# Moving where TensorE's operands start in SBUF, and the first bias rows and x loads of a two-block fp32 transformer kernel

## The chip, the cores and the metric

The kernel runs on one core of a Trainium2 chip, as one launch. The metric is device time in microseconds, median of three runs: 2502.96 us (2500.68 to 2505.42) before the change.

## The reference

Two transformer blocks run one after the other on a stream `x` of 256 tokens by 1024 features, all in float32. The first block is one layer: three groups of dilated window attention and a state-space scan side by side, gated and merged, then a SwiGLU feed-forward of 2816 hidden features, then a last norm. The second block is two layers with a second stream `xc` of 256 context tokens; each layer has a feed-forward, an attention mixer over both streams, and another feed-forward, with shifts, scales and gates from a modulation of `c`.

```python
h = x
h = h + hybrid_mixer(rmsnorm(h, norm1_w), ...)       # w_in gives q, k, v, z, xbc, dt, gates
h = h + swiglu(rmsnorm(h, norm2_w), w_ffn_in, w_ffn_out)
x = rmsnorm(h, final_norm_w)
...
for l in range(2):
    x = x + 0.5 * mx[2] * swiglu_2(modulate(rms_norm(x), ...), *ffn1)    # xc likewise
    y, y_c = mixer_l(h, hc, ...)
    x = x + mx[5] * y
    x = x + 0.5 * mx[8] * swiglu_2(modulate(rms_norm(x), ...), *ffn2)    # xc likewise, not in the last layer
```

In the dilated attention a bias is added to the logits before the softmax. It depends on the distance of query and key and on the head alone: `rel_bias[bucket(steps * dilation)]`, 24 heads, three groups of eight.

## The kernel before

**Products.** Features lie on the 128 partitions, tokens along the free axis. A weight slab of 128x1024 floats (eight blocks of 128 rows for 128 output features) is loaded by SP into `wraw` (`load_raw`, L111), rounded by ScalarE into `wh` (L120, type fp32r), and VectorE puts the rest, `wraw` minus `wh`, into `wl` (L121). Activations are split the same way into a high and a low part (`ah` and `al`, in the feed-forwards `hh` and `hl`). `mm3_k` (L134) then makes three products for each block of 128 rows: `wh` with high (L139), `wh` with low (L140), `wl` with high (L141). Weights are the stationary operand (loaded by PEld), activations the moving one. A slab is 24 products into one PSUM tile `pm`.

**Columns.** In the first block only `x` is there: 256 columns. From the second block on the two streams lie side by side in one tile (`self.comb`, `[128, KB, 2, T]`), so that a product takes 512 columns (`acts`, L143). The first three units of such a run, and some at its end, take each stream by itself, 256 columns of the same tile. In the last layer's second half only `x` is left: 256 columns again, of the `x` half of that tile.

**Order.** `run` (L197) takes a list of units and other work. It splits the weights of the coming units ahead (`prepare`), then emits products; the first `head` units are emitted as one batch, block by block. A scheduler orders the instructions of each engine from there, and every engine works through its own list in order. `wraw`, `wh` and `wl` have five buffers each, `pm` four. The dilated attention's units are woven with other work by `weave`.

**Bias rows.** At the start `onehot` (`oh`) and `rel_bias` (`rel`) are loaded by GpSimd's queue, three small products (L478) give a row of 896 values for each of eight heads (`brs`), and one GpSimd DMA writes this to DRAM 32 times over (`brow`, L480, 896 KB), so that `load_bias` (L511) can read it back with a row step one value shorter than a row: this gives the diagonal layout that the logits need. `load_bias` puts four DMAs for each group on SP's queue, the queue of the weights. `oh`, `rel` and `brs` lie in a pool that is closed at once, and the attention's tiles (`q`, `k`, the masks `mk`) take its place. `rpb` are eight more GpSimd DMAs (222 KB each, DRAM to DRAM) for the second layer's second mixer.

**Norm.** The norm's first step adds up squares of the eight blocks of `x` (L309 to L313), sums over partitions by TensorE (L336), takes a root on ScalarE (`rs`, L321), spreads it by TensorE (L344), and `y` (L357) is split into `ah` (L125) and `al` (L126).

**Addresses.** Pools take SBUF from the bottom up. `gap` (L92) takes a number of bytes and writes zeros to them, so that what follows starts elsewhere. In the program as built, the five `wraw` lie at 21696 and on, then `wh` from 42176 and `wl` from 62656, all tiles of 4096 bytes and so at 192 modulo 256 (a block of 128 columns is 512 bytes, which changes nothing). `ah` of the first block lies at 106880, of both streams at 115072, the hidden tiles at 147840 and on: 128 modulo 256, 64 bytes less. The normed scan output (`ynh`, `ynl`) is at 224.

## Time and profile before

| | |
|---|---|
| median of three runs | 2502.96 us (2500.68 to 2505.42) |
| profiled execution, its own time | 2511.2 us |
| its span, first to last instruction | 2509.1 us |
| mean granted TensorE clock | 0.986 |
| TensorE busy | 2440.5 us (97%) |
| weight loads (PEld) busy | 2097.5 us (84%) |
| VectorE busy | 1641.9 us (65%) |
| ScalarE busy | 1067.5 us (43%) |
| moved by DMA | 363.83 MB, mean 145 GB/s |

The table is one execution. A product's length in the trace runs from its issue to its last result; successive products overlap, so their rate is read from the distance of their starts. Times in the rows are counted from the start of the span.

### The profile page before, as it was taken

To read this page: it belongs to the slowest core of one execution; us is meant where nothing else is said; L and a number is where in the kernel's file an instruction comes from. 1 tells how busy PE (TensorE), PEld (TensorE's weight loads), DVE (VectorE), ACT (ScalarE), POOL (GpSimd) and SP (SyncE) were. 2 spreads that over 40 slices of the span, in tenths; PEclk is the share of its full clock that TensorE was granted. 3 is DMA by queue.
4 is the path that set the end of the run, shared out by engine and by line. 5 is a ranking of instruction groups with operands and counts; after the bars stand their busy time and mean duration, and the time that the engine had idled before them with its cause. 6 is when DMAs were issued, how large, how long until landed. Compare 5 with 4: busy or idle time off the path is not lost.

```text
span 2509.1 us, 38385 instructions
## 1 busy us (share of the span) xinstructions
PE 2440.5 (97%) x15104; PEld 2097.5 (84%) x15104; DVE 1641.9 (65%) x3012; ACT 1067.5 (43%) x1934; POOL 20.6 (1%) x30
## 2 busy tenths in 40 slices
PE   6999999999999999999999999999999999999999
PEld 5999899999888888886598888887888888866999
DVE  4667787787855675768757666657545455767555
ACT  4667565545522222536743222243222234555443
POOL 1000000000000000000000000000000000000000
PEclk9999899999999999999899999999999999999999
DMA  8555455676444554331025555434555422332554
GB/s 248 161 154 168 137 168 186 203 250 223 160 155 143 162 177 127 122 125 51 1 68 158 161 160 160 155 97 148 171 166 161 142 87 81 108 91 80 177 185 127
DMA packets 117252, 363.83 MB, mean 145 GB/s; under 512 B 21170, under 2 KB 28658, under 8 KB 117072
## 3 DMA queue, kind: packets, MB, share of 16 engines
q1 hardware_dynamic: 114512, 355.73, 44.8%
q0 software_dynamic: 1280, 3.45, 0.7%
q8 instruction: 119, 1.95, 0.3%
q10 hardware_dynamic: 1280, 2.20, 0.3%
q14 instruction: 61, 0.50, 0.1%
HBM read 359.33 MB, written 3.82 MB: 145 GB/s over the span
## 4 chain that ended last, share of the span: by engine, by line
PE 69%; DVE 4%; ACT 2%; issue 1%; DMA 0%; ACTq 0%; DVEq 0%; SPq 0%
PE pm L139 20%; PE pm L140 20%; PE pm L141 20%; PE pt L1128 1%; PE pa L1035 1%; DVE wl L121 1%; PE pm L1327 1%; PE pt L1059 1%; PE pa L1579 1%; PE pm L1587 1%; DVE al L362 1%; PE pa L1343 1%; DVE y L357 1%; PE pm L1267 1%; PE pa L1304 0%
## 5 line engine op out<-in xcount | busy, mean ns | idle before, releaser
L139 PE MATMUL pm<-ah,wh 128*128 128x256 f32 (+2 forms) x3096 | 1007.7, 328 | 25.3 <-ACT ah L361 11.0
L140 PE MATMUL pm<-al,wh 128*128 128x256 f32 (+2 forms) x3096 | 1001.8, 324 | 1.5 <-DVE al L362 1.5
L141 PE MATMUL pm<-ah,wl 128*128 128x256 f32 (+2 forms) x3096 | 999.9, 324 | 0.0
L120 ACT CAST wh<-wraw 128x1024 fp32r<-128x1024 f32 (+4 forms) x535 | 540.4, 1013 | 1028.8 <-PE pm L140 833.4
L121 DVE TENSOR_TENSOR wl<-wraw,wh 128x1024 fp32r<-128x1024 f32 (+4 forms) x535 | 627.4, 1176 | 245.9 <-ACT wh L120 243.4
L139 PEld LDWEIGHTS pm<-ah,wh 128*128 128x128 f32 (+1 forms) x3096 | 587.2, 191 | 87.4 <-ACT ah L361 12.5
L140 PEld LDWEIGHTS pm<-al,wh 128*128 128x128 f32 (+1 forms) x3096 | 591.2, 191 | 56.1 <-DVE al L362 2.8
L141 PEld LDWEIGHTS pm<-ah,wl 128*128 128x128 f32 (+1 forms) x3096 | 588.8, 190 | 52.9 <-issue 1.7
L140 PE MATMUL pm<-hl,wh 128*128 128x512 f32 (+1 forms) x934 | 316.5, 339 | 0.4 <-DVE hl L126 0.4
L139 PE MATMUL pm<-hh,wh 128*128 128x512 f32 (+1 forms) x934 | 316.0, 338 | 0.7 <-DVE xx L449 0.7
L141 PE MATMUL pm<-hh,wl 128*128 128x512 f32 (+1 forms) x934 | 315.9, 338 | 0.0
L989 DVE SCALAR_TENSOR_TENSOR junk<-wraw,cactc 128x1024 f32<-128x1024 f32 x112 | 137.1, 1224 | 187.7 <-DMA wraw<-w_mod 187.5
L989 DVE SCALAR_TENSOR_TENSOR junk<-wraw,cactx 128x1024 f32<-128x1024 f32 x144 | 176.0, 1222 | 40.9 <-DMA wraw<-w_mod 38.3
L140 PEld LDWEIGHTS pm<-hl,wh 128*128 128x128 f32 x934 | 176.4, 189 | 22.2 <-DVE hl L126 0.6
L139 PEld LDWEIGHTS pm<-hh,wh 128*128 128x128 f32 x934 | 175.7, 188 | 22.4 <-issue 0.8
L141 PEld LDWEIGHTS pm<-hh,wl 128*128 128x128 f32 x934 | 175.6, 188 | 21.5
L125 ACT CAST hh<-g 128x512 fp32r<-128x512 f32 (+1 forms) x113 | 59.3, 526 | 183.8 <-DVE g L419 183.8
L419 DVE TENSOR_TENSOR g<-g,pm 128x512 f32<-128x512 f32 (+1 forms) x113 | 64.0, 566 | 69.8 <-PE pm L141 67.9
L126 DVE TENSOR_TENSOR hl<-g,hh 128x512 fp32r<-128x512 f32 (+1 forms) x113 | 63.8, 566 | 0.3
L449 DVE SCALAR_TENSOR_TENSOR xc<-pm,mcol0c,xc 128x256 f32<-128x256 f32 x56 | 26.9, 481 | 56.0 <-PE pm L141 55.9
L415 ACT ACTIVATE g<-pm 128x512 f32<-128x512 f32 (+1 forms) x116 | 56.0, 487 | 1.4 <-PE pm L141 1.4
L1128 PEld LDWEIGHTS pt<-ident,e 128*128 128x128 f32 x272 | 30.7, 145 | 22.1 <-issue 18.8
(423 smaller groups left out, 2243.4 us busy)
## 6 DMA issues: line engine op xcount, KB each, us to landing
wraw<-w_mod SPq DMA_DIRECT2D x144, 512.0 KB, 3.9
wraw<-f1g SPq DMA_DIRECT2D x44, 512.0 KB, 3.7
wraw<-f1u SPq DMA_DIRECT2D x44, 512.0 KB, 4.2
wraw<-f2g SPq DMA_DIRECT2D x44, 512.0 KB, 3.7
wraw<-f2u SPq DMA_DIRECT2D x44, 512.0 KB, 4.0
wraw<-f1d SPq DMA_DIRECT2D x32, 512.0 KB, 4.2
wraw<-f2d SPq DMA_DIRECT2D x32, 512.0 KB, 3.6
wraw<-w_xbc SPq DMA_DIRECT2D x24, 512.0 KB, 3.6
```

The costliest lines, as they stand in the source:

```text
L120: nc.scalar.copy(h[:, :f], raw[:, :f])
L121: nc.vector.tensor_tensor(lo[:, :f], raw[:, :f], h[:, :f].bitcast(F32), op=ALU.subtract)
L125: self.nc.scalar.copy(h, src)
L126: self.nc.vector.tensor_tensor(lo, src, h.bitcast(F32), op=ALU.subtract)
L139: nc.tensor.matmul(out, h[:, c], ah, start=first, stop=False)
L140: nc.tensor.matmul(out, h[:, c], al, start=False, stop=False)
L141: nc.tensor.matmul(out, lo[:, c], ah, start=False, stop=last)
L415: nc.scalar.activation(half(g["g"], s), p, AF.Silu)
L419: nc.vector.tensor_tensor(t, t, p, op=ALU.mult)
L449: self.nc.vector.scalar_tensor_tensor(x, p, gate, x, op0=ALU.mult, op1=ALU.add)
L989: nc.vector.scalar_tensor_tensor(junk, raw, 1.0, K.cact[s], op0=ALU.mult, op1=ALU.mult, accum_out=K.mcol[layer, s][:, j:j + 1])
L1128: nc.tensor.transpose(p[:, j * 128:(j + 1) * 128], b, K.ident)
```

## The change

It does five things.

- *Addresses.* Both streams' `ah` and `al` get a gap of 64 bytes ahead and start at 192 modulo 256; the pools behind them move along, so that `hh` and `hl` come to 192 too. So the 4,770 products of 512 columns that have `wh` or `wl` (at 192) as weights go from distance 64 to distance 0. In the two feed-forwards that run on `x` alone (the first block's, and the last layer's second) a gap of 192 bytes more brings `hh` and `hl` back to 128, and for the second half of the last layer `self.alone` is a view of the activations' tile that starts 48 floats later, at 128. `ynh` and `ynl` come to 128.
- *Bias rows.* `oh` and `brs` are put into tiles that are used later (`bt`, `ct`). The three products are separate steps in the first `weave`; each group gets its own `brow` in DRAM, written 16 times over (192, 128 and 128 KB). `load_bias` issues eight DMAs of 16 partitions for each group, on GpSimd's queue.
- *x* (and later `xc`) comes in two DMAs of four blocks, one on SP's and one on ScalarE's queue, ahead of `cols` and `ident`.
- A first root of one column loads ScalarE's table for roots ahead of the squares; `na`, an exponential, moves into `dt_evac`.
- `run` prepares, for a run of one stream, one unit more while it stands at the first, and none at the last of the head.

```diff
+        self.gap(p, 64)
+        flat = [p.tile([128, KB * 2 * T], F32R, name="a" + n) for n in "hl"]
+        self.comb = [t.rearrange("p (b s t) -> p b s t", b=KB, s=2) for t in flat]
+        self.alone = [t[:, 48:48 + KB * T].rearrange("p (b t) -> p b t", b=KB) for t in flat]
...
     def new_act(self, s):
+        if self.single:
+            return tuple(self.alone)
...
-        for b in range(KB):
-            self.nc.sync.dma_start(self.X[s][:, b], src[:, b])
+        for b, e in ((0, self.nc.sync), (4, self.nc.scalar)):
+            e.dma_start(self.X[s][:, b:b + 4], src[:, b:b + 4])
...
             j, m = i, 0
+            if not two and i < head:
+
+                j = i + 1 if i + 1 < head else n
+                prepare(i)
...
-    brow = K.dram.tile([32, 8, 896], F32, name="brow")
-    for g, (c0, n) in enumerate(((0, 384), (384, 256), (640, 256))):
-        p = K.pa.tile([128, 512], F32, name="pa")
-        nc.tensor.matmul(p[:8, :n], rel[:, g * 8:(g + 1) * 8], oh[:, c0:c0 + n], start=True, stop=True)
-        nc.vector.tensor_copy(brs[:, c0:c0 + n], p[:8, :n])
-    nc.gpsimd.dma_start(brow.rearrange("q h u -> h q u"), brs.unsqueeze(1).to_broadcast([8, 32, 896]))
-    bctx.close()
+    brow = [K.dram.tile([16, 8, n], F32, name=f"brow{g}") for g, n in enumerate((384, 256, 256))]
...
+    oh, brs = (t.rearrange("p a t -> p (a t)")[:n, :896] for t, n in ((bt, 33), (ct, 8)))
+    nc.gpsimd.dma_start(oh, A["onehot"])
...
+    def bias_row(g):
+        c0, n = ((0, 384), (384, 256), (640, 256))[g]
+
+        def f():
+            p = K.pa.tile([128, 512], F32, name="pa")
+            nc.tensor.matmul(p[:8, :n], rel[:, g * 8:(g + 1) * 8], oh[:, c0:c0 + n], start=True, stop=True)
+            nc.vector.tensor_copy(brs[:, c0:c0 + n], p[:8, :n])
+            nc.gpsimd.dma_start(brow[g].rearrange("q h u -> h q u"), brs[:, c0:c0 + n].unsqueeze(1).to_broadcast([8, 16, n]))
+        return f
...
-        for a in range(0, 128, 32):
-            src = bass.AP(tensor=brow.tensor, offset=brow.offset + c0 + 127 - a, ap=[[8 * 896 - 1, 32], [896, 8], [1, w]])
-            nc.sync.dma_start(t[a:a + 32], src)
+        for a in range(0, 128, 16):
+            src = bass.AP(tensor=brow[g].tensor, offset=brow[g].offset + 127 - a, ap=[[8 * n - 1, 16], [n, 8], [1, w]])
+            nc.gpsimd.dma_start(t[a:a + 16], src)
...
-    items = weave(qkv_units(0), [start, lambda: load_bias(0)], 5, 4)
+    items = weave(qkv_units(0), [bias_row(0), start, bias_row(1), lambda: load_bias(0), bias_row(2)], 3, 2)
...
+    K.gap(K.pool(fctx, "gap1", 1), 192)
...
+        if layer == 1:
+            K.gap(K.pool(fctx, "gap2", 1), 192)
...
+    K.stream("x", A["x"])
     nc.scalar.dma_start(K.cols, A["cols"])
     nc.scalar.dma_start(K.ident, A["ident"])
-    K.stream("x", A["x"])
+
+    nc.scalar.activation(K.small.tile([128, 32], F32, name="v")[:, :1], K.ones[:, 0:1], AF.Sqrt)
```

ScalarE's list from its first weight casts on, before; `wh<-wraw` are casts of weights, `ah` of activations, `rs` is the norm's root and `q` the copy of the first finished product:

```order
L120 CAST wh<-wraw 128x1024 x2
L321 ACT_TABLE_LOAD
L321 ACTIVATE rs<-v 128x2
L120 CAST wh<-wraw 128x1024 x2
L125 CAST ah_230<-y 128x256 x4
L120 CAST wh<-wraw 128x1024
L125 CAST ah_230<-y 128x256 x4
L120 CAST wh<-wraw 128x1024 x4
L534 ACTIVATE q<-pm 128x256
```

And now:

```order
L120 CAST wh<-wraw 128x1024 x5
L330 ACTIVATE rs<-v 128x2
L125 CAST ah_213<-y 128x256 x6
L713 ACT_TABLE_LOAD
L713 ACTIVATE na<-cols 32x1
L125 CAST ah_213<-y 128x256 x2
L120 CAST wh<-wraw 128x1024
L545 ACTIVATE q<-pm 128x256
```

Five casts instead of two stand before the root, six instead of nine before the first copy of a product.

GpSimd's list of DMAs after the three loads, before:

```order
L1630 DMA rpb<-rpb 64x1x889
L480 DMA brow<-brs 8x32x896
L1630 DMA rpb<-rpb 64x1x889
L508 DMA mk_152<-mask 128x128
L508 DMA mk_154<-mask 128x128
L1630 DMA rpb<-rpb 64x1x889 x6
```

And now (`bias_502`, `bias_1434` and `bias_2308` are the three groups' bias tiles):

```order
L519 DMA mk_136<-mask 128x128
L519 DMA mk_138<-mask 128x128
L1643 DMA rpb<-rpb 64x1x889
L508 DMA brow_108<-ct 8x16x384
L508 DMA brow_109<-ct 8x16x256
L527 DMA bias_502<-brow_108 16x8x256 x8
L508 DMA brow_110<-ct 8x16x256
L527 DMA bias_1434<-brow_109 16x8x128 x8
L527 DMA bias_2308<-brow_110 16x8x128 x8
L1643 DMA rpb<-rpb 64x1x889 x7
```

The bias loads stood on SP's list, between the weights of the attention's units; that list now holds weights alone there.

## Rows read from the trace of the kernel before

**Rows 1.** the page's first part: busy time, share of the span and instructions

```profile
PE 2440.5 (97%) x15104; PEld 2097.5 (84%) x15104; DVE 1641.9 (65%) x3012; ACT 1067.5 (43%) x1934; POOL 20.6 (1%) x30
```

**Rows 2.** TensorE groups by shape: busy us, mean ns of one, idle before

```profile
L139 PE MATMUL pm<-ah,wh 128*128 128x256 f32 x1968 | 561.2, 288 | 25.3 <-ACT ah L361 11.0 <-ACT q L534 10.1 <-ACT ah L125 2.0
...
L139 PE MATMUL pm<-ah,wh 128*128 128x512 f32 x1112 | 441.6, 397 | 0.0
...
L139 PE MATMUL pm<-hh,wh 128*128 128x512 f32 x474 | 187.5, 396 | 0.0
...
L139 PE MATMUL pm<-hh,wh 128*128 128x256 f32 x460 | 128.5, 279 | 0.7 <-DVE xx L449 0.7
...
L139 PE MATMUL pm<-ynh,wh 128*128 128x256 f32 x96 | 26.9, 281 | 0.0
```

**Rows 3.** TensorE timeline, 256 columns, from 488 us: start, length

```profile
487.74 0.28 PE L141 MATMUL pm<-ah,wl 128*128 128x256 f32 x1
...
494.09 0.28 PE L140 MATMUL pm<-al,wh 128*128 128x256 f32 x1
```

**Rows 4.** the same, products of 256 columns from 2360 us

```profile
2359.79 0.28 PE L140 MATMUL pm<-al,wh 128*128 128x256 f32 x1
...
2366.38 0.28 PE L139 MATMUL pm<-ah,wh 128*128 128x256 f32 x1
```

**Rows 5.** the same, products of 512 columns from 850 us

```profile
849.74 0.40 PE L139 MATMUL pm<-ah,wh 128*128 128x512 f32 x1
...
862.80 0.40 PE L141 MATMUL pm<-ah,wl 128*128 128x512 f32 x1
```

**Rows 6.** timeline of TensorE round its first long wait

```profile
30.67 0.28 PE L141 MATMUL pm<-ah,wl 128*128 128x256 f32 x1
41.08 0.58 PE L139 MATMUL pm<-ah,wh 128*128 128x256 f32 x1 [10.13 <-ACT q L534]
...
45.09 0.35 PE L139 MATMUL pm<-ah,wh 128*128 128x256 f32 x1
```

**Rows 7.** timeline of ScalarE in that wait: idle before, and what ended it

```profile
34.48 1.04 ACT L120 CAST wh<-wraw 128x1024 fp32r<-128x1024 f32 x1 [11.86 <-DMA wraw<-w_k]
...
39.70 1.04 ACT L120 CAST wh<-wraw 128x1024 fp32r<-128x1024 f32 x1 [0.66 <-DMA wraw<-w_v]
40.65 0.38 ACT L534 ACTIVATE q<-pm 128x256 f32<-128x256 f32 x1
```

**Rows 8.** DMA issues, first 44 us: count, KB each, us to landing

```profile
wraw<-w_k SPq DMA_DIRECT2D x5, 512.0 KB, 10.2
...
rpb<-rpb POOLq DMA_DIRECT2D x8, 222.2 KB, 8.8
xx<-x SPq DMA_DIRECT2D x8, 128.0 KB, 5.3
...
brow<-brs POOLq DMA_DIRECT2D x1, 896.0 KB, 22.3
```

**Rows 9.** waits in the first 75 us: us in total, times, longest

```profile
POOL mk L508 <- DMA brow<-brs: 21.7, 1, 21.7
```

**Rows 10.** stretches from the start: busy us, then granted clock, DMA share, GB/s

```profile
32.00:42.00 10.00, 0.92 (x4) 0.92 (x5) 4.90 (x4) 5.28 (x8) 4.53 (x8) 0.65 0.84 300
42.00:52.00 10.00, 10.00 (x77) 10.00 (x77) 2.45 (x3) 3.27 (x5) 0.00 (x0) 0.84 1.06 282
52.00:62.00 10.00, 10.00 (x91) 10.00 (x90) 4.10 (x4) 4.43 (x8) 0.00 (x0) 1.00 1.02 292
```

**Rows 11.** timeline of all engines up to the first product

```profile
11.24 1.04 ACT L120 CAST wh<-wraw 128x1024 fp32r<-128x1024 f32 x1 [0.56 <-DMA wraw<-w_q]
...
14.89 0.20 ACT L321 ACTIVATE rs<-v 128x2 f32<-128x2 f32 x1
...
17.58 1.22 PE L139 MATMUL pm<-ah,wh 128*128 128x256 f32 x4 [1.01 <-ACT ah L125]
```

**Rows 12.** the tile bias: durations, first and last start

```profile
L576 DVE TENSOR_TENSOR pa<-pa,bias x8: 285/292/300, 70.6 to 96.0; 128x128 f32<-128x128 f32 x8
```

More of the change, by code (lines that the diff above doesn't have):

```diff
@@ L79, in __init__ @@
         self.small = self.pool(ctx, "small", 2)
-        self.comb, self.one_p = None, None
+        self.comb, self.one_p, self.single = None, None, False
         self.ps = ctx.enter_context(tc.tile_pool(name="ps", bufs=4, space=PSUM))
@@ L155, in stream @@
         self.X[s] = self.pool(self.ctx, "act" + s, 1).tile([128, KB, T], F32, name="x" + s)
-        for b in range(KB):
-            self.nc.sync.dma_start(self.X[s][:, b], src[:, b])
+        for b, e in ((0, self.nc.sync), (4, self.nc.scalar)):
+            e.dma_start(self.X[s][:, b:b + 4], src[:, b:b + 4])
     def both_acts(self):
         p = self.pool(self.ctx, "acts", 1)
-        self.comb = [p.tile([128, KB, 2, T], F32R, name="a" + n) for n in "hl"]
+        self.gap(p, 64)
+        flat = [p.tile([128, KB * 2 * T], F32R, name="a" + n) for n in "hl"]
+        self.comb = [t.rearrange("p (b s t) -> p b s t", b=KB, s=2) for t in flat]
+        self.alone = [t[:, 48:48 + KB * T].rearrange("p (b t) -> p b t", b=KB) for t in flat]
     def new_act(self, s):
+        if self.single:
+            return tuple(self.alone)
         if self.comb:
@@ L463, in linear @@
         return K.lin(src, i, K.acts, lambda s, p: evac(p), m)
-    bctx = ExitStack()
-    bp = K.pool(bctx, "b1b", 1)
-    oh = bp.tile([33, 896], F32, name="oh")
-    nc.gpsimd.dma_start(oh, A["onehot"])
-    rel = bp.tile([33, 24], F32, name="rel")
-    nc.vector.memset(rel, NEG)
-    nc.gpsimd.dma_start(rel[:32], A["rel_bias"])
-    brs = bp.tile([8, 896], F32, name="brs")
-    brow = K.dram.tile([32, 8, 896], F32, name="brow")
-    for g, (c0, n) in enumerate(((0, 384), (384, 256), (640, 256))):
-        p = K.pa.tile([128, 512], F32, name="pa")
-        nc.tensor.matmul(p[:8, :n], rel[:, g * 8:(g + 1) * 8], oh[:, c0:c0 + n], start=True, stop=True)
-        nc.vector.tensor_copy(brs[:, c0:c0 + n], p[:8, :n])
-    nc.gpsimd.dma_start(brow.rearrange("q h u -> h q u"), brs.unsqueeze(1).to_broadcast([8, 32, 896]))
-    bctx.close()
+    rel = xpool.tile([33, 24], F32, name="rel")
+    nc.vector.memset(rel, NEG)
+    brow = [K.dram.tile([16, 8, n], F32, name=f"brow{g}") for g, n in enumerate((384, 256, 256))]
     tri = K.cst.tile([128, 128], F32, name="tri")
-    nc.gpsimd.dma_start(tri, A["tri"])
     cw = xpool.tile([128, 128], F32, name="cw")[:, :120]
-    K.gap(xpool, 160)
+    K.gap(xpool, 320)
     K.gap(xpool, 352)
@@ L495, in block1 @@
     ao_l = xpool.tile([128, 4, T], F32R, name="aol")
+    K.gap(xpool, 192)
     mst = xpool.tile([128, 3, 2, 8], F32, name="mst")
@@ L498, in block1 @@
     big = lambda name: xpool.tile([128, 8, T], F32, name=name, tag="big")
+    oh, brs = (t.rearrange("p a t -> p (a t)")[:n, :896] for t, n in ((bt, 33), (ct, 8)))
+    nc.gpsimd.dma_start(oh, A["onehot"])
+    nc.gpsimd.dma_start(rel[:32], A["rel_bias"])
+    nc.gpsimd.dma_start(tri, A["tri"])
+    def bias_row(g):
[6 more added lines that the diff above has]
+        return f
     DIL = (1, 4, 16)
@@ L511, in load_bias @@
     def load_bias(g):
[L512 removed]
+        w, n = ((256, 384), (128, 256), (128, 256))[g]
         t = bias[g] = big("bias0") if g == 0 else hp.tile([128, 8, w], F32, name=f"bias{g}", tag="bias", bufs=2)
[L514 to L516 removed]
+        for a in range(0, 128, 16):
+            src = bass.AP(tensor=brow[g].tensor, offset=brow[g].offset + 127 - a, ap=[[8 * n - 1, 16], [n, 8], [1, w]])
+            nc.gpsimd.dma_start(t[a:a + 16], src)
         if g:
@@ L696, in block1 @@
     ladr = K.dram.tile([2, 32, 128], F32, name="ladr")
-    na = xpool.tile([32, 1], F32, name="na")
     def dt_evac(p):
@@ L701, in dt_evac @@
         v, u, w, c = (K.t1(n, (32, T)) for n in ("dv", "du", "dw", "dc"))
+        na = K.t1("na", (32, T))[:, 0:1]
         nc.scalar.activation(na, K.col("a_log", 0, slice(0, 32)), AF.Exp)
@@ L1536, in outputs @@
     def outputs():
+        K.single = True
         K.ACT["x"] = K.new_act("x")
```

1 line of the change is left out of this document (removed).

## The prediction

> **What bounds the kernel now.** I read the page's first part, then TensorE's groups by shape, then its timeline in steady stretches, then the waits of the first 75 us. TensorE is busy 97% of the span [rows 1]. Nearly all of it is one pattern, three products for each block of 128 rows: `wh` with the high part of the activations (L139), `wh` with the low part (L140), `wl` with the high part (L141). Counting each line three times, [rows 2] give (1112 + 474) x 3 = 4,758 products of 512 columns, and thousands of 256 columns. A length there is from issue to drain, and the products overlap, so what counts is the distance between starts. Each of [rows 3 to 5] shows the first and the last of 57 successive rows, 56 steps apart: (494.09 - 487.74) / 56 = 113.4 ns for 256 columns, (2366.38 - 2359.79) / 56 = 117.7 ns for 256 columns elsewhere, and (862.80 - 849.74) / 56 = 233.2 ns for 512 columns. No engine is waited for in these stretches: 256 columns have two levels with the same operand distance, and 512 have one.
>
> What would be free of any stall? After the first long wait, 19 products of 256 columns start from 41.08 to 45.09 us, 211 ns apart [rows 6], while the granted clock is 0.84 over the ten microseconds that hold them [rows 10]: the lower level, 1.2 GHz, at which 256 columns one a cycle take 213 ns. So at 2.4 GHz 512 columns need 213.3 ns, and the 233.2 hold 20 ns of something else; 256 columns need 106.7 and hold 6.7 or 11.0.
>
> The second bound is local. TensorE stands still from 30.67 + 0.12 to 41.08 us, 10.3 us, and the release is the copy of a finished product, `q` [rows 6]. It is not ScalarE's speed: `q` stands in ScalarE's queue behind four weight casts, the first of which waited 11.86 us for a weight transfer [rows 7]. Weights take 10.2 us to land then, since one `brow` write of 896 KB takes 22.3 us among them [rows 8]; GpSimd stands 21.7 us behind it [rows 9].
>
> **The change, part by part.** The sum is made against the profiled execution, 2511.2 us (span 2509.1), which lies 8.2 us over the median of the three runs, 2502.96; a difference found in the one is taken off the other.
>
> *The start.* The `brow` write becomes three (16 copies in place of 32: 192 + 128 + 128 KB, half the bytes), the bias loads go from SP's queue to GpSimd's, seven of the eight `rpb` writes go behind them, and on ScalarE three of the nine casts that stood before the first `q` come after it (the order rows in the section on the change). Also `q`'s tile no longer lies over `brs`, so it waits for no `brow` write. I expect the hole to close: minus 10.3 us. With it goes the slow clock behind it: 19 products at 211 instead of 117.7 ns, minus 1.8 us. Against that, the root `rs` now stands behind five casts instead of two, and each cast waits for its weights. Before, the first cast began at 11.24 and `rs` ran at 14.89 [rows 11]. Now x and four weights (3 MB) are asked for at once; at the 300 GB/s of a saturated stretch [rows 10] they and the small tables (0.8 MB) land by about 13.5 us, and the fifth weight near 15, so `rs` comes near 16.1 and the first product at 18.8 instead of 17.58: plus 1.2 us, an estimate from these rows (bounds: minus 1, since the table load before `rs` is gone too, and plus 3). Together minus 10.9. If the weights stay as late as before, there is nothing left of it: the bounds are 0 and minus 13.
>
> What is queued behind the moved work? On GpSimd only `rpb` (needed in the second layer). The first use of `bias0` is at 70.6 us [rows 12], and its eight loads can start once a 192 KB write is done; a 222 KB write took 8.8 us [rows 8]. Over 30 us of cover is left. The loads share the DMA engines with the weights, but at 52 to 62 us these were full (1.02, 292 GB/s) and TensorE was busy throughout [rows 10]. The four x loads fewer on each queue, the earlier table load and the small memsets lie before the first product or beside TensorE's work: nothing.
>
> *512 columns.* Addresses are no part of a trace; they follow from the tile sizes (the section on the kernel adds them up). Before, `wh` and `wl` lie at 192 modulo 256 and the activations at 128, 64 bytes below. Gaps move the activations and the hidden tiles to 192: distance 0. No product of the trace has distance 0, so the cost is bounded from the nearest rows. Floor: 213.3 ns, minus 20 ns each, 95 us in all. The 256-column rows give the closer bounds: one and the same product costs 113.4 or 117.7 ns, a matter of how the reads of the running product and of the next weights fall together; the 512's 233.2 is near two of the slow ones (235.4) and far from two fast ones (226.8). So what a better fall can give is seen to be 4.3 ns for a product, up to 6.4; what a worse one costs, by the same measure, is plus 4.3. I take minus 4.3: this shape has always been at its slow side, at this distance it never shows its fast one in 4,758 products, so a change of distance has more room below than above. 4,758 x 4.3 = minus 20.5 us. All of it is on the path, since TensorE waits for nobody there.
>
> The Trainium skill (TensorE: Matmul & The Clock Gate, Back-to-back issue gap) puts the distance of two products of N columns at N / 2.4 + 2.5 ns, 215.8 for 512. The trace disagrees for these operands: 233.2 [rows 5]. By that figure 17.4 ns a product, 83 us in all, would be there for the taking; I don't build on it.
>
> *256 columns.* Those that work beside 512-column ones (first and last units of two-stream stages) share their tiles and go to distance 0 as well: 2,580 products, counted in the program as built. The other distance in the trace, 32 bytes (`ynh`, 281 ns long [rows 2], the length of the slow level, against 276 of the fast), shows no fast level. I take them to the slow level, from half at each: 2,580 x 2.15 = plus 5.5 us (bounds: minus 11, plus 11). The single-stream products stay 64 bytes apart, where chance holds them at either level; the `ynh` ones join them (288 products, under 1 us).
>
> Sum: -10.9 - 20.5 + 5.5 = -25.9; 2502.96 - 25.9 = 2477.
>
> **The rivals.**
> 1. *Distance is nothing to 512 columns.* For it: one level, 233.2 ns, wherever I looked. Against it: the 256's two levels. Only the start pays, and the 256 stay too: 2503 - 10.9 = 2492. The Trainium skill (TensorE: Matmul & The Clock Gate, Step-by-step: what each phase is for) speaks for this rival: TensorE has two independent read ports, and loading the next weights takes nothing from the running product. By that rule no gap would matter; the two levels of [rows 3, 4] are hard to fit to it, though they don't refute it for 512.
> 2. *Distance 0 is the worst.* Both reads start at one residue and stay in each other's way. For it: they start together, and TensorE's weight loads take part in every step. Price: 4.3 ns more for each 512 and all 2,580 at the slow level or beyond (11 us): +20.5 + 11 - 10.9 = +20.6, 2524. It ends slower than before once a 512-column product costs (10.9 - 5.5) / 4,758 = 1.1 ns more, that is over 234.3 ns.
> 3. *The whole stall goes at distance 0*: at 222 ns (half of the 20 removed, and 256 columns unharmed), 4,758 x 11.2 = 53; 2503 - 53 - 10.9 = 2439.
> 4. *The start keeps its hole*, since half of the `brow` bytes, bias loads and weights still meet in the first 35 us and five casts stand before `rs`: 2477 + 10.9 = 2488.
>
> **How the numbers follow.** Forecast 0.42, rivals 0.24, 0.15, 0.12 and 0.07. The forecast's own range is 2462 (6.4 ns, start at its best) to 2490. The 80% range reaches to half of rival 3 and just beyond no change: 2442 to 2506. What a measurement of this kernel can tell is 0.2%, 5 us. Faster by more than that: 0.41 of the forecast, 0.20 of rival 1, all but 0.01 of rival 3, 0.05 of rival 4, 0.01 of rival 2: 0.78. Slower: 0.13 of rival 2 and 0.01 of the rest, 0.14. The remaining 0.08 is no change.
>
> **What would show it.** The distance of starts of 512-column products in a stretch without waits: near 229 ns (forecast), 233 (rival 1), over 234.3 (rival 2), 222 (rival 3). The 256-column ones of two-stream stages near 117.7. At the start: no wait of TensorE for `q`, first product by 19 us, granted clock 1.00 from 22 us on. `brow` landing in under 10 us each. I would be wrong most if 512 columns were slower: then everything that the start gives is lost within one feed-forward stage.

## The result, and the profile after

The changed kernel takes 2472.57 us (median of 4 runs, 2468.46 to 2473.19), the kernel before, beside it, 2504.19 (4 runs, 2500.68 to 2507.26): a ratio of 0.9861, 95% interval 0.9842 to 0.9880, or 31.6 us less. 2477 was forecast, with 2442 to 2506 as the range. The profiled execution took 2473.19 us, its span 2471.4; that of before had a span of 2509.1, so the two traces differ by 37.7 us, 6 us more than the medians. Where these 6 us come from is part of what follows.

The page's first part of the changed kernel (busy time, share of the span, instructions) answers to [rows 1], and shows TensorE as full as before:

```profile
PE 2415.3 (98%) x15104; PEld 2101.6 (85%) x15104; DVE 1642.8 (66%) x3016; ACT 1064.7 (43%) x1934; POOL 34.3 (1%) x56
```

TensorE's groups by shape, as in [rows 2]: the 512-column products became shorter (391 and 389 ns from issue to drain, against 397 and 396), and no wait for `q` is left among the releasers:

```profile
L139 PE MATMUL pm<-ah,wh 128*128 128x256 f32 x1968 | 563.3, 290 | 13.1 <-ACT ah L370 10.7 <-ACT ah L125 2.4
...
L139 PE MATMUL pm<-ah,wh 128*128 128x512 f32 x1112 | 434.7, 391 | 0.0
...
L139 PE MATMUL pm<-hh,wh 128*128 128x512 f32 x474 | 184.4, 389 | 0.0
```

The distance of starts, read as in [rows 3 to 5]: first and last of 57 successive rows (start, length) of TensorE's timeline in the changed kernel, in three stretches: products of 256 columns that read the two streams' tile (at 469 us this is the first block's feed-forward, where `x` alone stands in that tile), products of 512 columns, and the last feed-forward, where [rows 4] stand in the kernel before.

```profile
468.79 0.28 PE L140 MATMUL pm<-al,wh 128*128 128x256 f32 x1
...
475.51 0.28 PE L139 MATMUL pm<-ah,wh 128*128 128x256 f32 x1
...
839.82 0.39 PE L140 MATMUL pm<-al,wh 128*128 128x512 f32 x1
...
852.51 0.39 PE L139 MATMUL pm<-ah,wh 128*128 128x512 f32 x1
...
2329.82 0.28 PE L141 MATMUL pm<-ah,wl 128*128 128x256 f32 x1
...
2336.16 0.28 PE L140 MATMUL pm<-al,wh 128*128 128x256 f32 x1
```

Divided by 56: 120.0 ns for 256 columns at distance 0, a level that the kernel before does not have; 226.6 ns for 512 columns at distance 0, where [rows 5] give 233.2; 113.2 ns in the last stage, where [rows 4] give 117.7. Over all undisturbed steps, product by product between the two traces: 512 columns 233.32 to 226.79 ns (4,727 steps, -30.9 us), 256 columns in the two streams' tile 114.74 to 119.83 (2,364 steps, +12.0 us), the last feed-forward 117.78 to 113.33 (1,336 steps, -5.9 us), the other ones 115.57 to 114.64 (3,552 steps, -3.3 us).

The 233.3 ns are a mean. In the kernel before, nearly every step of 512 columns is either 230 to 231 ns long (2,327 of 4,757) or 235 to 236 (2,336), by turns; in the changed kernel 4,623 of 4,757 are 226 or 227 ns.

The start. TensorE's timeline up to the first product, which answers to [rows 6, 11]:

```profile
15.59 1.02 PE L345 MATMUL pt<-ones,acc 128*128 128x1 f32 x4 [3.78 <-DVE acc L322]
18.07 1.22 PE L353 MATMUL pt<-ident,rs 128*128 128x128 f32 x4 [1.47 <-DVE rs L331]
20.31 1.01 PE L139 MATMUL pm<-ah,wh 128*128 128x256 f32 x3 [1.01 <-ACT ah L125]
```

VectorE's timeline in the same stretch (start, length, and in brackets the idle time before and what ended it): its first real operation waits for the table of columns, the sum of squares is finished behind two weight splits, and only then come `v` and the root.

```profile
9.19 0.22 DVE L908 TENSOR_SCALAR cw<-cols 128x120 f32<-128x120 f32 x1 [7.78 <-DMA cols<-cols]
...
13.99 1.21 DVE L121 TENSOR_TENSOR wl<-wraw,wh 128x1024 fp32r<-128x1024 f32 x1
15.12 0.41 DVE L322 TENSOR_TENSOR acc<-acc,sq 128x256 f32<-128x256 f32 x1
...
16.64 0.16 DVE L329 TENSOR_SCALAR v<-pt 128x2 f32<-128x2 f32 x1
```

ScalarE's timeline, which answers to [rows 7]: the root `rs` behind the fifth cast, and the first `q` behind one more cast that waited for no transfer.

```profile
15.32 1.04 ACT L120 CAST wh<-wraw 128x1024 fp32r<-128x1024 f32 x1 [0.21 <-DMA wraw<-w_q]
16.83 0.20 ACT L330 ACTIVATE rs<-v 128x2 f32<-128x2 f32 x1 [0.47 <-DVE v L329]
...
30.54 1.05 ACT L120 CAST wh<-wraw 128x1024 fp32r<-128x1024 f32 x1 [5.21 <-issue]
31.50 0.38 ACT L545 ACTIVATE q<-pm 128x256 f32<-128x256 f32 x1
```

The DMA issues of the first 44 us (count, KB each, median us to landing), to be held against [rows 8]: the pieces of `brow` land in 9.2 and 8.2 us instead of 22.3, while weights take about as long as before.

```profile
wraw<-w_k SPq DMA_DIRECT2D x6, 512.0 KB, 10.3
...
brow<-ct POOLq DMA_DIRECT2D x2, 128.0 KB, 8.2
...
brow<-ct POOLq DMA_DIRECT2D x1, 192.0 KB, 9.2
```

Two stretches of the changed kernel (busy time of each engine, then granted clock, DMA share, GB/s): no slow clock at the start [rows 10], but one at 240 us, where the attention groups are combined.

```profile
38.00:48.00 10.00, 10.00 (x87) 10.00 (x87) 4.04 (x4) 4.10 (x7) 5.18 (x10) 1.00 1.06 245
...
240.00:245.00 5.00, 5.00 (x18) 3.93 (x17) 2.25 (x6) 1.22 (x4) 0.00 (x0) 0.51 0.43 151
```

The following table sets all traces side by side. It is worked out from the start times of the 12,738 products of L139 to L141, numbered from 0: when the first starts and when number 700 starts (the start is over by then), how long numbers 1,500 to 1,800 take (the combining stage), 5,000 to 11,400 (nearly all two-stream, 512 columns with their 256-column edges), and 11,400 to 12,700 (the last feed-forward). In us.

| kernel | first | no. 700 | 1,500-1,800 | 5,000-11,400 | 11,400-12,700 |
|---|---|---|---|---|---|
| before | 17.6 | 127.1 | 58.7 | 1589.1 | 153.1 |
| changed | 20.3 | 119.0 | 63.8 | 1563.3 | 147.3 |
| start_alone | 20.4 | 118.1 | 63.6 | 1590.9 | 153.1 |
| both_shift | 20.5 | 119.6 | 63.2 | 1564.0 | 147.3 |
| tail_zero | 20.6 | 119.1 | 63.4 | 1567.2 | 156.0 |
| cols_first | 20.7 | 118.8 | 53.0 | 1564.7 | 147.3 |
| before_own | 17.5 | 137.1 | 63.7 | 1590.8 | 153.1 |
| before_16 | 18.1 | 118.0 | 61.7 | 1596.3 | 147.3 |
| copies32 | 20.6 | 130.3 | 63.8 | 1564.0 | 147.3 |
| own_zero | 17.3 | 137.0 | 63.5 | 1564.0 | 147.3 |
| spread | 20.3 | 119.4 | 56.8 | 1564.9 | 153.1 |
| spread_x8 | 16.7 | 120.7 | 51.9 | 1565.6 | 153.1 |
| gap288 | 20.4 | 119.9 | 55.6 | 1592.0 | 151.2 |
| gap352 | 20.5 | 120.1 | 60.1 | 1591.9 | 153.8 |

The fourth column has two values, 1563 to 1567 for every kernel with 512 columns at distance 0 and 1589 to 1596 for every other: 26 us, which is the gain of the 512 columns less the loss of the 256-column edges. The third and the last column move by 5 to 11 us between kernels with the same code there: neither the addresses nor the code of the stage settle that part of a trace. It is called chance below, though with one trace for each kernel the runs don't show whether it changes from one execution to the next.

### The profile page after: what moved, and what is told of

Same layout as the page of the kernel before. It is cut to its first block, busy times and chain, and to the rows that moved or that the text cites. A ratio compares the mean times of both kernels' runs of the same rounds, so it can differ in the third digit from the quotient of the medians.

```text
span 2471.4 us, 38395 instructions
## 1 busy us (share of the span) xinstructions
PE 2415.3 (98%) x15104; PEld 2101.6 (85%) x15104; DVE 1642.8 (66%) x3016; ACT 1064.7 (43%) x1934; POOL 34.3 (1%) x56
## 4 chain that ended last, share of the span: by engine, by line
PE 70%; DVE 3%; ACT 2%; issue 1%; DMA 0%; ACTq 0%; DVEq 0%
PE pm L139 20%; PE pm L140 20%; PE pm L141 20%; PE pt L1140 1%; PE pa L1047 1%; PE pm L1339 1%; PE pt L1071 1%; PE pa L1592 1%; DVE wl L121 1%; PE pm L1600 1%; PE pa L1355 1%; PE pm L1279 1%; PE pa L1316 0%; PE pm L1622 0%; PE pm L1165 0%
## 5 line engine op out<-in xcount | busy, mean ns | idle before, releaser
L139 PE MATMUL pm<-ah,wh 128*128 128x256 f32 (+2 forms) x3096 | 1002.9, 326 | 13.1 <-ACT ah L370 10.7
L141 PE MATMUL pm<-ah,wl 128*128 128x256 f32 (+2 forms) x3096 | 996.1, 322 | 0.0
L139 PEld LDWEIGHTS pm<-ah,wh 128*128 128x128 f32 (+1 forms) x3096 | 590.1, 192 | 67.8 <-ACT ah L370 12.3
L141 PEld LDWEIGHTS pm<-ah,wl 128*128 128x128 f32 (+1 forms) x3096 | 592.2, 191 | 46.6 <-issue 2.3
L139 PE MATMUL pm<-hh,wh 128*128 128x512 f32 (+1 forms) x934 | 312.1, 334 | 0.0
L141 PE MATMUL pm<-hh,wl 128*128 128x512 f32 (+1 forms) x934 | 312.1, 334 | 0.0
L139 PEld LDWEIGHTS pm<-hh,wh 128*128 128x128 f32 x934 | 175.7, 188 | 18.7
L141 PEld LDWEIGHTS pm<-hh,wl 128*128 128x128 f32 x934 | 175.8, 188 | 18.4
L428 DVE TENSOR_TENSOR g<-g,pm 128x512 f32<-128x512 f32 (+1 forms) x113 | 64.0, 567 | 55.6 <-PE pm L141 54.1
```

Source lines behind the costliest of these rows:

```text
L139: nc.tensor.matmul(out, h[:, c], ah, start=first, stop=False)
L141: nc.tensor.matmul(out, lo[:, c], ah, start=False, stop=last)
L428: nc.vector.tensor_tensor(t, t, p, op=ALU.mult)
```

## The experiments

Twelve kernels ran, each beside the kernel before on the same chip. The median of before was 2513 there for gap288, gap352, spread and spread_x8 and 2507 for the other eight, so ratios are compared, not times.

**The start without the addresses.** Operands 64 bytes apart again:

```diff
-        self.gap(p, 64)
-    K.gap(K.pool(fctx, "gap1", 1), 192)
-        K.single = True
-        if layer == 1:
-            K.gap(K.pool(fctx, "gap2", 1), 192)
```

> The changed kernel with the operands put back 64 bytes apart everywhere (512 and 256 columns); the new start stays. Theory (start and addresses add up): 512-column products start 233.3 ns apart again instead of 226.75, so 4,758 x 6.55 = +31 us; the 2,580 two-stream 256-column ones go from 119.8 back to about 115.7, -10.6; the 1,770 products of the last feed-forward from 113.3 to 117.7, +7.8; together 2472.6 + 28 = about 2501, and the start alone is worth 3 to 8 us against the kernel before. Rival 1 (the whole gain is the start's, distance is nothing): 2473. Rival 2 (the start gives nothing): 2504 and TensorE still waits 10 us for a copy of q.

Measured: 2502.82 us (12 runs, 2497.34 to 2510.61), ratio 0.9985, interval 0.9970 to 1.0000. TensorE's timeline, 57 rows of 512 columns:

```profile
849.78 0.39 PE L140 MATMUL pm<-al,wh 128*128 128x512 f32 x1
...
862.85 0.39 PE L139 MATMUL pm<-ah,wh 128*128 128x512 f32 x1
```

233.4 ns again. Against the changed kernel's 0.9861 the addresses are worth 0.0124 of the time, 31 us, and the start alone 4 us of the median, with an interval that reaches to no change. Product 700 starts 9.0 us earlier than before, but the combining stage takes 4.9 us longer: in this trace the start gives 9, and half of it is gone after that stage.

**Distance or place.** A gap of 64 bytes ahead of the weights too:

```diff
+        self.gap(self.pool(ctx, "gap0", 1), 64)
         self.raw_p = self.pool(ctx, "raw", 5)
```

> The changed kernel with every operand, weights and activations alike, 64 bytes further on: all distances stay (0 for 512 columns, 64 for single-stream 256), but the residue of 192 modulo 256 becomes 0. Theory (the distance decides): 512-column products 226.75 ns apart, 2472.6 us within 5. Rival (the place of each operand decides): about 233 ns, 2472.6 + 31 = 2504, or some other pace than 226.75.

Measured: 2479.53 us (4 runs, 2468.62 to 2486.60), ratio 0.9884, interval 0.9851 to 0.9918, which overlaps that of the changed kernel. The 512-column products start 226.8 ns apart (mean over 4,757 steps) with both operands at residue 0 instead of 192. So the distance decides, not the place.

**Other distances.** The gap between the weights and everything else changed from 320 bytes; in the first kernel the last stage also got its activations back at blocks of 2,048 bytes, 64 from the weights:

```diff
-        self.gap(self.pool(ctx, "gap", 1), 320)
+        self.gap(self.pool(ctx, "gap", 1), 288)
-        self.alone = [t[:, 48:48 + KB * T].rearrange("p (b t) -> p b t", b=KB) for t in flat]
+        self.alone = [t.rearrange("p (b r) -> p b r", b=KB)[:, :, 56:56 + T] for t in flat]
```

> The changed kernel with all other tiles 32 bytes nearer to the weights: 512-column and two-stream 256-column products at distance 32, single-stream 256 at 96, but the last stage's activations at 64 with blocks 2,048 bytes apart as in the kernel before (the changed kernel has 1,024). For reading the distances of starts only. Theory (512 columns gain at 0 alone because both reads then fall together): 233 ns at 32. Rival (a distance under 64 is enough): 226.75 at 32. For the last stage: 117.7 ns if the 2,048-byte stride is what holds it at the slow level, 113.3 if the level hangs on the moment at which the stage begins.

```diff
-        self.gap(self.pool(ctx, "gap", 1), 320)
+        self.gap(self.pool(ctx, "gap", 1), 352)
```

> The changed kernel with all other tiles 32 bytes farther from the weights: 512-column and two-stream 256-column products at distance 224 (32 below the next 256), single-stream 256 at 32. For reading the distances of starts only. Theory (pace depends on the distance alike to both sides of 0): 512 columns as at 32. Rival (it is the order of the two reads that counts): another pace than at 32, 226.75 on one side and 233 on the other. 256 columns at 32: 119.8, 117.7 or 113.3 ns shows where the third level begins.

Measured, one run each: 2508.16 and 2515.82 us. 57 rows of 512 columns at distance 32:

```profile
849.81 0.40 PE L141 MATMUL pm<-ah,wl 128*128 128x512 f32 x1
...
862.88 0.40 PE L140 MATMUL pm<-al,wh 128*128 128x512 f32 x1
```

and at distance 224:

```profile
849.78 0.39 PE L140 MATMUL pm<-al,wh 128*128 128x512 f32 x1
...
862.85 0.39 PE L139 MATMUL pm<-ah,wh 128*128 128x512 f32 x1
```

233.4 ns at both, as at 64: of the four distances tried, 0 alone is faster for 512 columns, and 32 bytes to either side lose all of it. 256 columns: 118.3 ns at 32, 118.0 at 96, 117.0 at 224 (trimmed means over 500 to 2,400 steps), 119.8 at 0; 113.3 held over long stretches at 64 alone. In the last stage of gap288, at distance 64 and with the stride of before, both levels occur (1,300 steps, mean 116.3). The stride does not hold it at one.

**The last stage at distance 0.**

```diff
-        K.single = True
-        if layer == 1:
-            K.gap(K.pool(fctx, "gap2", 1), 192)
```

> The changed kernel without the separate view for the last single-stream stage, whose 1,770 products of 256 columns go from distance 64 to distance 0. Theory (distance decides, 0 is a level of its own for 256 columns): 119.8 instead of 113.3 ns, 1,770 x 6.5 = +11.5, 2484 us. Rival 1 (distance 0 is the slow one of the two levels): 117.7, +7.8, 2480. Rival 2 (the last stage runs at 113.3 by chance and the view is nothing to it): 113.3 or 117.7 whatever the distance, 2473 to 2480, 119.8 nowhere in this stage.

Measured: 2489.94 us (6 runs, 2475.30 to 2491.92), ratio 0.9920, interval 0.9896 to 0.9944: 0.0059 over the changed kernel, 15 us; 11.5 was expected. TensorE's timeline there, 57 rows:

```profile
2344.74 0.28 PE L141 MATMUL pm<-ah,wl 128*128 128x256 f32 x1
...
2351.46 0.28 PE L140 MATMUL pm<-hl,wh 128*128 128x256 f32 x1
```

120.0 ns, as expected. The separate view of the last stage earns its place: without it, part of what the 512 columns gain would be paid back here.

**The table of columns first.** To bring the first product forward:

```diff
+    nc.scalar.dma_start(K.cols, A["cols"])
     K.stream("x", A["x"])
-    nc.scalar.dma_start(K.cols, A["cols"])
     nc.scalar.dma_start(K.ident, A["ident"])
```

> The changed kernel with the table of columns asked for ahead of the second half of x on ScalarE's queue, so that VectorE's first real operation, cw, which waits for it to 9.19 us, runs at about 4.6. Theory A (two things in a row hold the first product: VectorE's late sums and the five weight casts ahead of the root rs; the fifth cast ends at 16.36): rs moves from 16.83 to about 16.4 and the first product from 20.31 to about 19.8, the time by -0.5 us, not to be told from nothing. Theory B (the late table alone made the start later than before): the first product returns to 17.6, -2.8 us, 2470.

Measured: 2474.71 us (5 runs, 2464.72 to 2480.23), ratio 0.9862, interval 0.9838 to 0.9887. The first product came at 20.73 us, not at 19.8 and not at 17.6: neither theory. `cw` ran at 6.09, but the second half of x, now second on that queue, kept ScalarE's squares waiting until 9.67, where the changed kernel's went on without a wait, and the last two additions of squares still stood behind two weight splits. What this trace shows instead is the combining stage. The windows of that stretch:

```profile
240.00:245.00 5.00, 5.00 (x30) 3.69 (x29) 3.98 (x12) 1.20 (x3) 0.00 (x0) 1.00 0.46 144
245.00:250.00 5.00, 5.00 (x27) 3.49 (x26) 3.58 (x10) 2.03 (x4) 0.00 (x0) 1.00 0.28 102
```

The granted clock is 1.00 where the changed kernel has 0.51, TensorE starts 30 instructions in five microseconds instead of 18, with the same order and a wait of the same 1.1 us ahead of it. The stage takes 53.0 us instead of 63.8. This execution was the shortest of its five, 2464.72. Another of the five, at the same mean granted clock of 0.990, took 2474.71 us, so more than the clock differs from one execution to the next.

**Why the hole closed.** Three kernels. First, the kernel before with half the bytes in `brow` and nothing else of the change, so that `q` stays behind nine casts:

```diff
-    brow = K.dram.tile([32, 8, 896], F32, name="brow")
+    brow = K.dram.tile([16, 8, 896], F32, name="brow")
-    nc.gpsimd.dma_start(brow.rearrange("q h u -> h q u"), brs.unsqueeze(1).to_broadcast([8, 32, 896]))
+    nc.gpsimd.dma_start(brow.rearrange("q h u -> h q u"), brs.unsqueeze(1).to_broadcast([8, 16, 896]))
-        for a in range(0, 128, 32):
+        for a in range(0, 128, 16):
```

> The kernel before with brow in 16 copies instead of 32: one write of 448 KB instead of 896, loads in steps of 16 rows; the order on ScalarE stays, q behind nine casts. Theory T (bytes among the weights make them late): the write lands in about 11 us instead of 22.3, weights in 8 instead of 10.2, and the hole of 10.3 us shrinks to 4 or less: -6 to -12 us. Theory O (the order): the ninth weight is asked for as late as before (24.85 us), and the hole stays at 8 to 10 us, the time within 3 us of the kernel before.

Measured: 2499.23 us (10 runs, 2486.37 to 2510.58), ratio 0.9970, interval 0.9949 to 0.9990. The waits of TensorE, first 80 us (us in total, times, longest), then the DMA issues of `brow` and of weights, first 44 us:

```profile
PE pm L139 <- ACT q L534: 1.3, 1, 1.3
```

```profile
wraw<-w_k SPq DMA_DIRECT2D x5, 512.0 KB, 8.8
...
brow<-brs POOLq DMA_DIRECT2D x1, 448.0 KB, 12.0
```

The wait for `q` goes from 10.1 to 1.3 us [rows 6], and product 700 starts 9.1 us earlier, with the order on ScalarE untouched. The weights land sooner: 9.2, 8.8 and 7.7 us for `w_q`, `w_k` and `w_v`, where the kernel before has 10.0, 10.2 and 12.1. Second, the changed kernel with the old 896 KB in its three pieces:

```diff
-    brow = [K.dram.tile([16, 8, n], F32, name=f"brow{g}") for g, n in enumerate((384, 256, 256))]
+    brow = [K.dram.tile([32, 8, n], F32, name=f"brow{g}") for g, n in enumerate((384, 256, 256))]
-            nc.gpsimd.dma_start(brow[g].rearrange("q h u -> h q u"), brs[:, c0:c0 + n].unsqueeze(1).to_broadcast([8, 16, n]))
+            nc.gpsimd.dma_start(brow[g].rearrange("q h u -> h q u"), brs[:, c0:c0 + n].unsqueeze(1).to_broadcast([8, 32, n]))
```

> The changed kernel with 32 copies of each of the three brow pieces instead of 16, 896 KB in all as in the kernel before; loads still take 16 of the 32. Order on ScalarE as in the changed kernel (q behind six casts). Theory T (bytes): weights land later by some us and TensorE waits 3 to 6 us for q again, 2476 to 2479. Theory O (order): no wait for q over 1 us, 2473 within what runs differ.

Measured: 2487.37 us (4 runs, 2484.53 to 2495.07), ratio 0.9933, interval 0.9912 to 0.9953: 0.0072 over the changed kernel, 18 us. TensorE's waits from 30 to 75 us, then a DMA issue of weights, first 44 us:

```profile
PE pt L553 <- ACT v L545: 5.7, 1, 5.7
```

```profile
wraw<-w_k SPq DMA_DIRECT2D x5, 512.0 KB, 12.4
```

The hole is back, later, at 50 us, for `v` instead of `q`, and the clock falls behind it (0.66 from 50 to 60 us); product 700 starts 11.3 us later than in the changed kernel. The weights take 12.4 to 12.6 us to land here, against 10.1 to 10.8 in the changed kernel. The pieces alone, with the old bytes, don't close the hole. Third, the kernel before with `brs` and the one-hot table in tiles that are used later, so that `q` stands behind six casts instead of nine; the lines that write `brow` move below these tiles, and the transfers stay as they were:

```diff
-    oh = bp.tile([33, 896], F32, name="oh")
-    brs = bp.tile([8, 896], F32, name="brs")
+    oh, brs = (t.rearrange("p a t -> p (a t)")[:n, :896] for t, n in ((bt, 33), (ct, 8)))
```

> The kernel before with one edit: the one-hot table and the brs rows lie in tiles that are used later (bt, ct), as in the changed kernel, so that q's tile no longer lies over brs. The brow write stays one piece of 896 KB, the bias loads stay on SP's queue, x in eight loads, distances 64. ScalarE's queue then has six casts ahead of the first q instead of nine. Theory O (the hole came from the order: q behind four more casts, the last of a weight asked for at 24.85 us): TensorE's wait for q of 10.3 us goes, as does the slow clock behind it, and the time falls by about 12 us, 2507 to 2495. Theory T (that of the prediction: weights land late because the 896 KB brow write lies among them): the write still takes about 22 us, the casts still wait some 12 us, and the time stays within 3 us of the kernel before.

Measured: 2527.92 us (5 runs, 2525.28 to 2528.63), ratio 1.0088, interval 1.0072 to 1.0104: slower than before, which no theory had. TensorE's timeline at its two holes:

```profile
36.97 0.58 PE L139 MATMUL pm<-ah,wh 128*128 128x256 f32 x1 [5.33 <-ACT q L531]
...
87.48 0.47 PE L591 MATMUL pt<-ident,pr 128*128 128x128 f32 x1 [4.36 <-ACT pr L584]
```

With `q` behind six casts, as in the changed kernel, but the old transfers, half of the first hole stays; its cast still waits 13.87 us for a weight. The second hole is new: the scheduler now asks for the bias loads at 71.6 us instead of 42.4, first uses `bias0` at 85.3 instead of 70.6 [rows 12], and has run 135 more of the large products by then than the kernel before. Then the chain of bias, maximum, exponent and turn stands on TensorE's path with nothing beside it, and the granted clock is 0.50 from 90 to 100 us. The same start under the new addresses:

> The start of before_own (brs and the one-hot table in other tiles, all else of the start as in the kernel before: x in eight loads, columns first, root rs behind one cast) with the addresses of the changed kernel (512 columns at distance 0, last stage 64 apart). Theory (the first product of the changed kernel is 2.8 us late because x comes in two loads and the root stands behind five casts; the addresses give about 28 us wherever the start stands): first product at 17 us or before instead of 20.3, no wait for q, 2462 to 2468 us, 5 to 10 below the changed kernel. Rival (three pieces and GpSimd's queue for the bias loads are needed): the hole comes back and it is no faster than the changed kernel, 2473 or more.

Its edit is that of before_own and the address lines of the change. Measured: 2494.39 us (6 runs, 2491.96 to 2496.24), ratio 0.9955, interval 0.9939 to 0.9971. The first product comes at 17.3, but both holes are there (5.6 and 4.4 us) and product 700 starts 18 us later than in the changed kernel: the rival was right. Its fourth column is 1564.0; the addresses give their 26 us whatever the start.

**The combining stage.** The twelve small products of the stage, two behind each unit of 24 large ones:

```diff
-    items += weave(z_units[2] + z_units[3],
-                   [lambda: combine_turn(0), lambda: combine_turn(1), lambda: combine_turn(2), combine_weights]
-                   + sum([[lambda b=b: combine(b)] for b in range(4)], []) + scan0[:2])
+    parts = [lambda b=b, g=g: combine(b, g) for b in range(4) for g in range(3)]
+    for u in z[2:] + [gate_unit(2), gate_unit(3)]:
+        items += [u] + ([] if u in z[2:4] else [parts.pop(0), parts.pop(0)])
```

> The changed kernel with the twelve small products that combine the attention groups (8 rows, L669) spread out, two after each 24 large products (two gate products are computed earlier to make room), instead of all within some 60 products. Theory C (the granted clock falls to its lower level for 14 to 25 us in that stage in nine of the ten profiles so far, and in the one where it stayed up, cols_first, the stage took about 11 us less): the clock stays at 1.00 through 235 to 265 us and the time falls by 8 to 11 us, 2462 to 2465. Rival (the fall has another cause, or comes later once the small products are farther apart): the stage has as much time at the lower clock as before, 2470 to 2476.

Measured: 2475.99 us (5 runs, 2463.75 to 2481.79), ratio 0.9856, interval 0.9824 to 0.9889: not to be told from the changed kernel. The windows show that the clock falls all the same, for less time in the stage (14 us against 24), and once more later:

```profile
240.00:245.00 5.00, 5.00 (x19) 3.94 (x18) 2.65 (x5) 1.03 (x2) 0.00 (x0) 0.50 0.24 95
...
290.00:295.00 5.00, 5.00 (x37) 5.00 (x37) 3.54 (x9) 2.76 (x6) 0.00 (x0) 0.76 0.34 122
```

Theory C did not hold as it was put: the clock falls with the small products spread, as it stayed up in cols_first with them crowded. Whether the spread shortens the fall is left open by one trace of each kernel. TensorE's timeline in the last stage of the same kernel, 57 rows:

```profile
2344.77 0.28 PE L139 MATMUL pm<-hh,wh 128*128 128x256 f32 x1
...
2351.36 0.28 PE L141 MATMUL pm<-hh,wl 128*128 128x256 f32 x1
```

117.7 ns, at the very addresses at which the changed kernel has 113.2. So the addresses don't settle the level of the last stage, and what does is open. Last, the same with x in eight loads behind the columns:

```diff
-        for b, e in ((0, self.nc.sync), (4, self.nc.scalar)):
-            e.dma_start(self.X[s][:, b:b + 4], src[:, b:b + 4])
+        for b in range(KB):
+            self.nc.sync.dma_start(self.X[s][:, b], src[:, b])
```

> The same with x in eight loads on SP's queue behind the columns and the unit matrix, as in the kernel before, so that the root rs stands behind one weight cast instead of five. Theory (the first product of the changed kernel is late by VectorE's sums of squares and the root, both behind weight splits and casts): first product at 16.5 to 17.5 us instead of 20.3, no wait for q over 2 us, 3 us less than the kernel with the spread alone, 2459 to 2462. Rival (x in eight loads takes longer, and what the first product gains the next weights lose): a wait of TensorE of 3 us or more before 60 us and no gain.

Measured: 2475.26 us (5 runs, 2465.96 to 2478.62), ratio 0.9846, interval 0.9812 to 0.9880. TensorE's timeline at its start:

```profile
16.69 1.01 PE L139 MATMUL pm<-ah,wh 128*128 128x256 f32 x3 [1.01 <-ACT ah L125]
...
20.78 1.01 PE L139 MATMUL pm<-ah,wh 128*128 128x256 f32 x3 [1.97 <-ACT ah L125]
```

The first product does come 3.6 us earlier, as the theory had it, but it then waits for the next activations, and product 700 starts at 120.7, no earlier than in the changed kernel (119.0). The rival was right here too, with smaller waits than it named. In both spread traces the last stage ran at its slow level, 5.8 us longer than in the changed kernel's, which hides part of what the shorter combining stage gives (56.8 and 51.9 us against 63.8). By the medians none of these kernels beats the changed one by more than the runs differ.

## Why the prediction was right, and where its terms were off

The forecast went by two gains and one loss, and all three are there. Its sum, -25.9 against the -31.6 us measured, hides errors of both signs; that they nearly cancelled is luck.

| term | forecast | in the two traces |
|---|---|---|
| start, to product 700 | -10.9 | -8.1 |
| 512 columns to distance 0 | -20.5 | -30.9 |
| 256 columns in the two streams' tile to distance 0 | +5.5 | +12.0 |
| last stage | 0, by chance either level | -5.9, by chance |
| combining stage | not seen | +5.1, by chance |

Other steps add up to the remaining 9.9 us of the 37.7 between the traces, 3.3 of them products at distance 64 that fell to the faster level more often, and the rest short waits that I did not follow; some 4 us of them lie in the first block's feed-forward, where the trace of before has 4.7 us of steps beyond the usual between products 3,300 and 3,900 and that of the changed kernel 0.4. The last stage's 5.9 is about what the traces differ by beyond the medians; that it accounts for it is argued, not shown.

**512 columns.** The sign held: the room was below, not above. The size did not: I took 4.3 ns, the difference of the two levels of 256 columns; it was 6.5, the other bound that I had named (two fast 256-column products, 226.8, against 226.79 measured). Part of this is luck. That 512 columns have more room below than above says nothing of why distance 0 should give it, and at that distance 256 columns went to their worst, so what the one shape does is no measure of the other. I gave as the reason how the reads of the running product and of the next weights fall together; no run shows the reads, only that the pace depends on the distance. The "one level" of 233.2 ns was also the mean of two steps, 231 and 236, which 57 rows taken as one don't show. That distance is the cause, and not the place or the start, is shown by start_alone (233.4), both_shift (226.8 at residue 0) and the kernels at 32 and 224 (233.4). Rival 1, that distance is nothing to 512 columns, is refuted, and so is rival 2; rival 3's 222 ns was not reached. The Trainium skill (TensorE: Matmul & The Clock Gate, Step-by-step: what each phase is for) has loading the next weights take no read bandwidth from the running product. With the same instructions, 32 bytes between the two addresses cost 6.6 ns of 233 here, which is hard to fit to that rule, though no run shows which read waits.

**256 columns.** I moved them to the slow level of the two that the trace shows, 117.7, because a third had not been seen. Distance 0 has one of its own, 119.8 to 120.0, and it is steady. The sign was right, the size was half. The prediction also had all 2,580 of these products beside 512-column ones. But 1,056 of them are the first block's feed-forward, whose `ah` and `al` lie in the two streams' tile though `x` is alone there: in that stage 1,018 steps go from 114.1 to 119.9 ns, 5.9 of the 12.0 us. The change brought only `hh` and `hl` back to distance 64 in it (113.4 ns). A view like `self.alone` there would by these levels (113.3 or 117.8) save an estimated 2 to 7 us; no run tried it. What I said of the products that stay 64 bytes apart, that they can be at either level whatever the addresses, is what spread and the changed kernel show at equal addresses (117.7 and 113.2), and before_16 against before (147.3 and 153.1 us for the last stage).

**The start.** The hole and the slow clock behind it went as forecast, and the cause was the one named: before_16 closes the hole by the bytes alone and copies32 opens one by the bytes alone. Rival 4, that the hole stays, is refuted. In those two kernels the weights land sooner with fewer bytes (7.7 to 9.2 us) and later with more (12.4 to 12.6), as the prediction had it; in the changed kernel their time to landing stayed at 10.1 to 10.8 us, against 10.0 to 12.1 before. The order has a share too: before_own, with `q` behind six casts and the old bytes, keeps 5.3 of the 10.1 us. In the changed kernel the eighth weight is asked for at 19.22 us instead of 23.39, `q` stands behind six casts, and ScalarE waits 2.2 us for a weight at most between 20 and 48 us, where it waited 11.86 before. The first product was forecast at 18.8 and came at 20.31, within the bounds (plus 3) but for another reason than mine. I had `rs` wait for the fifth cast; it waited for `v`, because VectorE finished the sum of squares at 15.5, behind the column table, the three copies of bias rows and two weight splits. I counted ScalarE's queue ahead of the root and left out VectorE's, on which the same splits stand. The forecast's "granted clock 1.00 from 22 us on" held to 240 us. The 211 ns that the prediction gives the slow products is off a little: 19 rows have 18 steps, and the steady ones among them are 213 ns.

**What was missing** is the combining stage. The clock falls there in 13 of the 14 traces, for 3 to 24 us (worked out from the granted clock of five-microsecond windows), and the stage takes 51.9 to 63.8 us. The kernel before spent 14 us there at the lower clock, the changed one 24; a trace of before alone shows one draw of it. Part of the start's gain is given back in this stage in the traces of start_alone and the changed kernel. An earlier start is not what costs it: before_own, copies32 and own_zero reach product 700 later than the kernel before and lose 24 us there too, and cols_first, with the same order there and a start as early as the changed kernel's, lost nothing. What makes the clock fall is open too; that the small products stand close together is not enough.

## What to carry to other kernels

Where TensorE is full and a weight load stands between any two products, look at the byte distance between the moving operand and the next weights modulo 256, in steady stretches, by the distance of starts and not by length; for each shape measure the distances that the tiles can have, since of the distances tried here 0 is the best for 512 columns and the worst for 256. Give every stage that has only the one shape its own view of the tiles, and list which stages read a shared tile before moving it. A large write beside the weights can hold TensorE up though TensorE does not wait for that write, and moving one consumer forward in its queue without it may open a hole elsewhere.

## What the runs showed of the hardware

- Distance of starts by shape and distance modulo 256: 512 columns 226.8 ns at 0 and 233.3 at 32, 64 and 224; 256 columns 119.8 at 0, 118.3 at 32, 113.3 or 117.8 at 64, 118.0 at 96, 117.0 at 224. Worked out at 2.4 GHz, the means are 544 and 560 cycles for 512 columns and 272 (113.3) to 288 (120.0) for 256. A mean can hide unequal steps: at 64 the steps of 512 columns are 231 and 236 ns by turns, at 32 they are 232 to 235, at 0 all but a few are 226 or 227. At 1.2 GHz, 256 columns start 213 ns apart in the combining stage, without an excess.
- At distance 64 the level of 256 columns can be held for a whole stage, 1,300 products, and differs between kernels with the same addresses and code there: 113.2 and 117.7 ns in the last stage, 5.8 us. In gap288 it changed within that stage.
- The granted clock of one stage can stay at its upper level in one kernel and fall for over 20 us in another with the same instructions on TensorE there: 53.0 against 63.8 us. This is as large as the whole start, and lies inside what runs of one kernel differ by (2464.72 to 2480.23 us in cols_first).
